# Two-block transformer kernel on one core: where the big SBUF tiles start, and how far apart the weight buffers lie

## Chip, cores and metric

The kernel runs on 1 core of one Trainium2 chip. The metric is the device time of one launch in microseconds (us). Three runs of the kernel before took 925.46, 927.27 and 922.51 us; the median is 925.46 us.

## What is computed

256 tokens of width 1024 pass through two different transformer blocks, all in float32. Cut to what matters here:

```python
def reference(x, ...):
    # block 1: sliding-window attention (8 heads) and retention (4 heads), gated, then an MLP
    proj = rmsnorm(x) @ w_in
    ...
    h = x + (ga * (y_a @ w_att_up) + gr * (y_r @ w_ret_up)) @ w_out
    x = rmsnorm(h + square(relu(rmsnorm(h) @ w_ff1)) @ w_ff2)
    # block 2: 16 meta tokens in front; windowed attention (16 heads) and differential attention
    ...
    h = h + rms_norm((g_swa * (o_swa @ w_bs) + g_diff * (o_diff @ w_bd)) @ w_out_2)
    u = rms_norm(h)
    return h + rms_norm((silu(u @ w_gate) * (u @ w_up)) @ w_ffn_out)
```

There are some 36 million weights. They are used once each, so the kernel is one long stream of weights past a small set of activations.

## The kernel before

**Units.** The host packs all weights, in the order of their use, into 272 units of 128 partitions x 1024 float32 (512 KB each). `fetch` (L285 to L302) brings in one unit. SyncE's queue loads it into a tile `raw` (4 buffers). ScalarE copies it into `hi` (L299, two pieces of 512 columns), rounded to the format fp32r, and VectorE writes the remainder `lo = raw - hi` (L301, two pieces). `hi` and `lo` have five buffers each (`WB = 5`), taken in turn. `next_unit` keeps one unit ahead of the one in use. A few units go into big activation tiles that are free at that time (`spare`), and are then called `w`.

**Products.** Activations are kept split in the same way: a big tile such as `x1t` holds, for each of 8 slices k of the contraction, a hi part and a lo part. One product is three fp32r matmuls (`PASS`): hi by hi, hi by lo, lo by hi. A matmul has a stationary operand, which a weight load brings into the array (128 columns, 512 bytes in each partition), and a moving operand, which streams past it. There are two large kinds:

- `mm_a` (L454): the unit's 128x128 slices are stationary and 256 token columns of the activation move (1,024 bytes in each partition; 272 columns in block 2's attention, with the meta tokens). 24 matmuls per unit. Its activations are `x1t`, `xf1t`, `x2t`, `xf2t`, `ret_t`, `oa_t`, `os_t`, `od_t`.
- `mm_b` (L466): 128 tokens of the activation are stationary (`m1t`, `m2t`, `hid`) and 512 columns of the unit move (2,048 bytes). 12 matmuls per unit. `mm_group` (L476) does the same for a group of four units.

A slice k of a big tile follows the last at 1,024 bytes. Only `x2t` has 272 columns to a slice, so that its slices follow at 1,088 bytes.

Transposes go through TensorE too (L433, L580, L961 and others), with the data as stationary and a 128x128 identity as the moving operand. A few products (L689 to L691, L973 to L975) are in plain float32.

**SBUF.** The pools stand one behind the other in each partition: `const` (small tables, `vec` among them), `w` (the weight buffers), `big` (the big activation tiles), `small`, and then one pool per phase. A pool rounds a tile's size up to 32 bytes. So the size of `vec`, 40 floats or 160 bytes, sets where all that comes behind it starts. `consts2` (L361) makes `vec`, and borrows a `raw` buffer for the masks (L364).

**Order.** The scheduler of the framework sets the order of each engine's instructions; the change leaves it as it is.

Of the kernel before, what the change touches and what calls it, by code (L numbers as in the profile page):

```python
# [9 lines left out]
F32 = mybir.dt.float32  # L10
F32R = mybir.dt.float32r
# [5 lines left out]
P = 128  # L17
# [5 lines left out]
EPS = 1e-6  # L23
MASKED = 1e30
UC = 1024

RET_H = 4

# [2 lines left out]
WB = 5  # L31
# [192 lines left out]
class Body:  # L224
# [59 lines left out]
    def fetch(self):  # L284
        nc = self.nc  # L285
        u = self.un
        self.un += 1
        if u in self.place:
            hi, lo = self.place.pop(u)
        else:  # L290
            hi = self.wp.tile([P, UC], F32R, tag="hi", bufs=WB, name=f"hi{u}")
            lo = self.wp.tile([P, UC], F32R, tag="lo", bufs=WB, name=f"lo{u}")
        raw = self.wp.tile([P, UC], F32, tag="raw", bufs=4, name=f"raw{u}")
        nc.sync.dma_start(out=raw, in_=self.io["wstream"][u])
        if self.hi_pool:
            nc.gpsimd.tensor_scalar(out=hi, in0=raw, scalar1=1.0, scalar2=0.0, op0=ALU.mult, op1=ALU.add)
        else:
            for c in range(0, UC, PIECE):
                nc.scalar.copy(hi[:, c:c + PIECE], raw[:, c:c + PIECE])  # L299
        for c in range(0, UC, PIECE):  # L300
            nc.vector.tensor_sub(lo[:, c:c + PIECE], raw[:, c:c + PIECE], hi[:, c:c + PIECE].bitcast(F32))  # L301
        self.ready.append((hi, lo))  # L302

    def spare(self, skip, tags):

        u = self.un + skip
        for tag in tags:
            if tag == "DE":
                self.place[u] = [self.bp.tile([P, UC], F32R, tag="D", name=f"hi{u}"),
                                 self.bp.tile([P, UC], F32R, tag="E", name=f"lo{u}")]  # L310
# [50 lines left out]
    def consts2(self):  # L361
        nc, cp, io = self.nc, self.cp, self.io
        cc = _CC
        mk = self.wp.tile([P, UC], F32, tag="raw", bufs=4, name="mk")[:, 0:3 * P]  # L364
        a, n = cc["masks"]
        nc.sync.dma_start(out=mk, in_=io["consts"][:, a:a + n])
        self.identb = cp.tile([P, P], BF16, name="identb")
        self.masks = cp.tile([P, 3 * P], BF16, name="masksb")
        nc.gpsimd.tensor_copy(self.identb, self.ident)
        nc.gpsimd.tensor_copy(self.masks, mk)  # L370
        self.vec = cp.tile([P, 40], F32, name="vec")
        nc.sync.dma_start(out=self.vec, in_=io["vec"])
        self.hb = cp.tile([P, 32], F32, name="hb")
        nc.gpsimd.tensor_scalar(out=self.hb, in0=self.vec[:, 0:32], scalar1=0.5, scalar2=None, op0=ALU.mult)
        rb = cp.tile([P, 24 + 256 + P], F32, name="rows")
        nc.sync.dma_start(out=rb, in_=io["rows"].broadcast_to([P, 280 + P]))
        self.nsink = cp.tile([P, 24], F32, name="nsink")
        nc.gpsimd.tensor_scalar(out=self.nsink, in0=rb[:, 0:24], scalar1=-1.0, scalar2=None, op0=ALU.mult)
        self.sub = rb[:, 280:]
        nc.gpsimd.tensor_scalar(out=self.sub, in0=self.sub, scalar1=0.8, scalar2=None, op0=ALU.mult)  # L380
        lam4 = rb[:, 24:280].rearrange("p (a b d) -> p a b d", a=2, b=2)
        pr = cp.tile([P, 2, 64], F32, name="lampr")
        nc.gpsimd.tensor_tensor(out=pr, in0=lam4[:, :, 0, :], in1=lam4[:, :, 1, :], op=ALU.mult)
        s2 = cp.tile([P, 2], F32, name="lams")
        nc.vector.reduce_sum(out=s2, in_=pr, axis=AX.X)
        e2 = cp.tile([P, 2], F32, name="lame")
        nc.scalar.activation(out=e2, in_=s2, func=AF.Exp)
        self.nlam = cp.tile([P, 1], F32, name="nlam")
        nc.gpsimd.tensor_tensor(out=self.nlam, in0=e2[:, 1:2], in1=e2[:, 0:1], op=ALU.subtract)
        nc.gpsimd.tensor_scalar(out=self.nlam, in0=self.nlam, scalar1=-(0.8 - 0.6 * math.exp(0.0)), scalar2=None,  # L390
                                op0=ALU.add)
# [740 lines left out]
```

## Time and profile before

| | |
|---|---|
| median of 3 runs | 925.46 us (922.51 to 927.27) |
| profiled execution, its own time | 926.7 us |
| its span (first to last instruction) | 924.9 us |
| TensorE matmul busy (PE) | 896.0 us, 97% |
| TensorE weight load busy (PEld) | 819.9 us, 89% |
| VectorE busy (DVE) | 627.7 us, 68% |
| ScalarE busy (ACT) | 516.5 us, 56% |
| GpSimd busy (POOL) | 174.7 us, 19% |
| weights and tables from HBM | 151.83 MB, 166 GB/s over the span |

Matmuls are pipelined: one starts while the last is still under way, so the duration of one (283 ns for 256 columns) is longer than the distance from start to start. In this text that distance is called the *pitch*. It is read from the timeline: the start of one row, the start of a later row, and the number of matmuls between them. In a row of the timeline "x2" means two equal instructions in a run, with the start of the first.

### The profile page before, as it was taken

The numbers are of one execution on the slowest core, as the hardware profiler recorded it, in microseconds if no ns is written. First come the engines' busy times: TensorE is split into PE (matmuls) and PEld (weight loads), VectorE is DVE, ScalarE is ACT, GpSimd is POOL, SyncE is SP. The second block draws the span as 40 slices with busy tenths as digits, with TensorE's granted clock in tenths as the row PEclk, the third lists the DMA queues.
The fourth block names the chain that finished last, engine by engine and source line by source line (L and its number), as shares of the span: only waits on it lengthen the run. The fifth ranks groups of instructions, "written<-read, shape, count | busy, mean of one in ns | idle before, by whom it ended". The sixth has DMA issues, their size and how long they took to land. (4 is left out here: it accounts for less than half of the span.)

```text
span 924.9 us, 16482 instructions
## 1 busy us (share of the span) xinstructions
PE 896.0 (97%) x6188; PEld 819.9 (89%) x6188; DVE 627.7 (68%) x1201; ACT 516.5 (56%) x1128; POOL 174.7 (19%) x181
## 2 busy tenths in 40 slices
PE   6999899999999999999989999999999999999997
PEld 4898889998899999987989878899999799999996
DVE  5556789667755544575589999988567675655554
ACT  4544367555554445565557778886455464444442
POOL 3013460101001111001273534451011100000000
PEclk9999999999999999999999999999999999999999
DMA  8675544478565565662564333433466666666651
GB/s 280 232 207 167 154 150 137 123 220 294 174 209 190 185 182 183 189 220 94 189 207 135 110 110 127 138 109 115 136 184 209 224 206 191 189 190 182 183 159 45
DMA packets 48126, 160.18 MB, mean 173 GB/s; under 512 B 6432, under 2 KB 8224, under 8 KB 48048
## 3 DMA queue, kind: packets, MB, share of 16 engines
q1 hardware_dynamic: 43376, 153.95, 52.6%
q10 hardware_dynamic: 4672, 5.20, 2.0%
q8 instruction: 48, 0.79, 0.3%
q14 instruction: 30, 0.25, 0.1%
HBM read 151.83 MB, written 2.10 MB: 166 GB/s over the span
## 5 line engine op out<-in xcount | busy, mean ns | idle before, releaser
L301 DVE TENSOR_TENSOR lo<-raw,hi 128x512 fp32r<-128x512 f32 x536 | 380.5, 751 | 195.1 <-ACT hi L299 190.5
L299 ACT CAST hi<-raw 128x512 fp32r<-128x512 f32 x532 | 301.9, 618 | 244.3 <-issue 84.7
L466 PE MATMUL op<-hi,hid 128*128 128x512 f32 x416 | 131.1, 396 | 0.0
L454 PE MATMUL fi_ps<-xf2t,hi 128*128 128x256 f32 x640 | 115.7, 283 | 0.0
L454 PEld LDWEIGHTS fi_ps<-xf2t,hi 128*128 128x128 f32 x640 | 100.4, 192 | 1.0
L466 PEld LDWEIGHTS op<-hi,hid 128*128 128x128 f32 x416 | 76.4, 188 | 16.4
L454 PE MATMUL fi_ps<-xf2t,lo 128*128 128x256 f32 x320 | 90.5, 283 | 0.0
L466 PE MATMUL op<-lo,hid 128*128 128x512 f32 x208 | 82.0, 396 | 0.0
L454 PE MATMUL f_ps<-xf1t,hi 128*128 128x256 f32 x448 | 81.3, 283 | 0.0
L454 PEld LDWEIGHTS f_ps<-xf1t,hi 128*128 128x128 f32 x448 | 70.7, 191 | 1.4
L454 PE MATMUL f_ps<-xf1t,lo 128*128 128x256 f32 x224 | 63.3, 282 | 0.0
L454 PEld LDWEIGHTS fi_ps<-xf2t,lo 128*128 128x128 f32 x320 | 61.3, 192 | 0.0
L454 PE MATMUL q_ps<-x2t,hi 128*128 128x256 f32 x256 | 50.4, 287 | 0.4 <-ACT t L503 0.4
L454 PE MATMUL gate_ps<-x1t,hi 128*128 128x256 f32 x256 | 49.1, 287 | 0.0
L454 PE MATMUL gate_ps<-x2t,hi 128*128 128x256 f32 x256 | 48.7, 285 | 0.0
L466 PEld LDWEIGHTS op<-lo,hid 128*128 128x128 f32 x208 | 39.1, 188 | 9.4
L415 POOL TENSOR_SCALAR e<-ss 128x1 f32<-128x1 f32 (+1 forms) x11 | 4.0, 362 | 223.9 <-ACT py L1028 195.0
L795 POOL TENSOR_TENSOR sq<-relu 128x512 f32<-128x512 f32 x14 | 15.8, 1132 | 152.0 <-ACT relu L792 152.0
L454 PEld LDWEIGHTS f_ps<-xf1t,lo 128*128 128x128 f32 x224 | 42.8, 191 | 0.1
L454 PEld LDWEIGHTS q_ps<-x2t,hi 128*128 128x128 f32 x256 | 40.4, 189 | 1.5 <-ACT t L503 0.6
L454 PEld LDWEIGHTS gate_ps<-x2t,hi 128*128 128x128 f32 x256 | 40.0, 189 | 0.6 <-issue 0.5
L454 PEld LDWEIGHTS gate_ps<-x1t,hi 128*128 128x128 f32 x256 | 40.3, 191 | 0.2
(297 smaller groups left out, 2023.8 us busy)
## 6 DMA issues: line engine op xcount, KB each, us to landing
raw<-in_wstream_dram SPq DMA_DIRECT2D x272, 512.0 KB, 3.6
sw<-t ACTq DMA_DIRECT2D x40, 64.0 KB, 3.8
x<-in_x_dram SPq DMA_DIRECT2D x3, 512.0 KB, 6.0
sw<-t ACTq DMA_DIRECT2D x40, 34.0 KB, 2.4
sw<-t ACTq DMA_DIRECT2D x8, 128.0 KB, 5.0
g_pre<-in_gains_dram SPq DMA_DIRECT2D x2, 512.0 KB, 6.1
x<-hf SPq DMA_DIRECT2D x2, 512.0 KB, 2.8
x<-x SPq DMA_DIRECT2D x2, 512.0 KB, 6.1
```

The source lines that it names most:

```text
L299: nc.scalar.copy(hi[:, c:c + PIECE], raw[:, c:c + PIECE])
L301: nc.vector.tensor_sub(lo[:, c:c + PIECE], raw[:, c:c + PIECE], hi[:, c:c + PIECE].bitcast(F32))
L415: nc.gpsimd.tensor_scalar(out=e[:np_], in0=ss[:np_, 0:1], scalar1=1.0 / D, scalar2=EPS, op0=ALU.mult, op1=ALU.add)
L454: nc.tensor.matmul(out, wv[a][:, k, j * P:(j + 1) * P], XT[:, b, k, n0:n1], start=(i == 0), stop=(i == last))
L466: nc.tensor.matmul(out, XT[:, b, k0 + k, t0:t1], wv[a][:, k, c0:c0 + cn], start=(start and i == 0), stop=(stop and i == last))
L795: nc.gpsimd.tensor_tensor(out=q, in0=r, in1=r, op=ALU.mult)
```

## The change

`vec` gets 48 columns instead of 40 (the DMA still fills 40), so that everything behind it moves by 32 bytes. The weight buffers `hi`, `lo` and `raw` get 1,040 columns instead of 1,024, of which the first 1,024 are used, so that one buffer follows the next at 4,160 bytes instead of 4,096. Nothing else changes: in the built program the rows of all five engines, with their waits and buffer numbers, are the same as before, but for the line numbers (the lines behind L25 move down by one, those from L371 on by two).

```diff
 UC = 1024
+UP = UC + 16
...
         else:
-            hi = self.wp.tile([P, UC], F32R, tag="hi", bufs=WB, name=f"hi{u}")
-            lo = self.wp.tile([P, UC], F32R, tag="lo", bufs=WB, name=f"lo{u}")
-        raw = self.wp.tile([P, UC], F32, tag="raw", bufs=4, name=f"raw{u}")
+            hi = self.wp.tile([P, UP], F32R, tag="hi", bufs=WB, name=f"hi{u}")[:, 0:UC]
+            lo = self.wp.tile([P, UP], F32R, tag="lo", bufs=WB, name=f"lo{u}")[:, 0:UC]
+        raw = self.wp.tile([P, UP], F32, tag="raw", bufs=4, name=f"raw{u}")[:, 0:UC]
...
-        mk = self.wp.tile([P, UC], F32, tag="raw", bufs=4, name="mk")[:, 0:3 * P]
+        mk = self.wp.tile([P, UP], F32, tag="raw", bufs=4, name="mk")[:, 0:3 * P]
...
-        self.vec = cp.tile([P, 40], F32, name="vec")
-        nc.sync.dma_start(out=self.vec, in_=io["vec"])
+
+        self.vec = cp.tile([P, 48], F32, name="vec")
+        nc.sync.dma_start(out=self.vec[:, 0:40], in_=io["vec"])
```

The two programs' tables of addresses (bytes from the start of a partition; the remainders are what the text speaks of):

| tile | before | remainder by 64, by 256 | changed | remainder by 64, by 256 |
|---|---|---|---|---|
| `hi`, five buffers | 20704, 24800, 28896, 32992, 37088 | 32, 224 for all | 20736, 24896, 29056, 33216, 37376 | 0; 0, 64, 128, 192, 0 |
| `lo`, five buffers | 41184 to 57568, 4096 apart | 32, 224 for all | 41536 to 58176, 4160 apart | 0; 64, 128, 192, 0, 64 |
| `raw`, four buffers | 61664 to 73952, 4096 apart | 32, 224 for all | 62336 to 74816, 4160 apart | 0; 128, 192, 0, 64 |
| `x1t`, `xf1t`, `od_t` | 78048 | 32, 224 | 78976 | 0, 128 |
| `m1t`, `m2t`, `os_t` | 94432 | 32, 224 | 95360 | 0, 128 |
| `ret_t`, `x2t`, `xf2t` | 110816 | 32, 224 | 111744 | 0, 128 |
| `hid`, four places | 180768, 184864, 188960, 193056 | 32, 32 | 181696, 185792, 189888, 193984 | 0, 192 |
| `p` (five buffers), `a` (two) | 200864 and on, 1120 apart | 32 and 0 in turn | 201792 and on | 0 and 32 in turn |
| `ident` (transposes) | 16512 | 0, 128 | 16512 | 0, 128 |

While one matmul streams its moving operand, the weights of the next are loaded. The *distance* below is the address of a matmul's moving operand less that of the stationary operand loaded for the next one, its remainder by 256. Over the 5,691 matmuls in fp32r it stands so in the two programs:

| moving columns | program | 0 | 64 | 128 | 192 |
|---|---|---|---|---|---|
| 256 | before | 3325 | 210 | 200 | 259 |
| 256 | changed | 820 | 1045 | 1247 | 874 |
| 272 | before | 128 | 139 | 127 | 118 |
| 272 | changed | 134 | 125 | 106 | 116 |
| 512 | before | 454 | 33 | 0 | 657 |
| 512 | changed | 245 | 316 | 331 | 271 |

(The 272 wide rows have the odd difference at the ends of runs. A handful of narrower matmuls is not shown.) Before, the 256 wide ones at other distances than 0 are those of `x2t`, whose slices are 1,088 bytes apart and so go through all four distances; of the 512 wide ones at 192, 622 are those of `hid`.

## Rows read from the trace of the kernel before

**Rows 1.** The page: span and busy time of each engine.

```profile
span 924.9 us, 16482 instructions
PE 896.0 (97%) x6188; PEld 819.9 (89%) x6188; DVE 627.7 (68%) x1201; ACT 516.5 (56%) x1128; POOL 174.7 (19%) x181
```

**Rows 2.** Busy time by stretch, core 0: stretch, its us, busy us (instructions).

```profile
core 0: us, PE busy (x) PEld busy (x) DVE busy (x) ACT busy (x) POOL busy (x), PEclk, DMA share, GB/s
0.00:50.00 50.00, 41.18 (x218) 35.15 (x219) 27.61 (x45) 25.17 (x49) 9.51 (x19) 1.00 0.76 259
...
250.00:420.00 170.00, 170.00 (x1049) 150.93 (x1048) 95.05 (x153) 88.32 (x163) 17.29 (x18) 1.00 0.62 196
...
450.00:640.00 190.00, 182.41 (x1373) 166.27 (x1373) 170.15 (x375) 142.99 (x367) 88.86 (x77) 1.00 0.44 130
...
735.00:905.00 170.00, 169.95 (x1192) 158.54 (x1190) 101.11 (x185) 82.12 (x164) 0.00 (x0) 1.00 0.57 177
```

**Rows 3.** Timeline of PE, a stretch of `mm_a`, `xf2t` moving: start, us, what.

```profile
897.31 0.40 PE L454 MATMUL fi_ps<-xf2t,hi 128*128 128x256 f32 x2
897.55 0.28 PE L454 MATMUL fi_ps<-xf2t,lo 128*128 128x256 f32 x1
897.67 0.40 PE L454 MATMUL fi_ps<-xf2t,hi 128*128 128x256 f32 x2
...
902.71 0.40 PE L454 MATMUL fi_ps<-xf2t,hi 128*128 128x256 f32 x2
```

**Rows 4.** Timeline of PEld in the same stretch: the weight loads.

```profile
897.20 0.31 PEld L454 LDWEIGHTS fi_ps<-xf2t,hi 128*128 128x128 f32 x2
897.43 0.19 PEld L454 LDWEIGHTS fi_ps<-xf2t,lo 128*128 128x128 f32 x1
897.55 0.31 PEld L454 LDWEIGHTS fi_ps<-xf2t,hi 128*128 128x128 f32 x2
```

**Rows 5.** Timeline of PE, a stretch of `mm_a` with `x2t` moving.

```profile
671.85 0.40 PE L454 MATMUL gate_ps<-x2t,hi 128*128 128x256 f32 x2
672.09 0.28 PE L454 MATMUL gate_ps<-x2t,lo 128*128 128x256 f32 x1
672.21 0.40 PE L454 MATMUL gate_ps<-x2t,hi 128*128 128x256 f32 x2
...
676.47 0.40 PE L454 MATMUL gate_ps<-x2t,hi 128*128 128x256 f32 x2
```

**Rows 6.** Timeline of PE, `mm_b` with `m2t` stationary.

```profile
719.44 0.61 PE L466 MATMUL op<-hi,m2t 128*128 128x512 f32 x2
719.89 0.39 PE L466 MATMUL op<-lo,m2t 128*128 128x512 f32 x1
...
724.20 0.61 PE L466 MATMUL op<-hi,m2t 128*128 128x512 f32 x2
```

**Rows 7.** Timeline of PE, `mm_b` with `hid` stationary.

```profile
275.95 0.63 PE L466 MATMUL op<-hi,hid 128*128 128x512 f32 x2
276.42 0.39 PE L466 MATMUL op<-lo,hid 128*128 128x512 f32 x1
...
280.85 0.63 PE L466 MATMUL op<-hi,hid 128*128 128x512 f32 x2
```

**Rows 8.** Timeline of PE, `mm_group` with `x2t` stationary, 512 columns moving.

```profile
424.68 0.39 PE L476 MATMUL vb_ps<-hi,x2t 128*128 128x512 f32 x1
...
427.67 0.39 PE L476 MATMUL vb_ps<-lo,x2t 128*128 128x512 f32 x1
```

**Rows 9.** Two tiles' instructions: duration ns min/median/max, first and last start.

```profile
L961 PEld LDWEIGHTS at_ps<-ident,a x32: 138/141/143, 589.4 to 654.2; 128*128 128x128 f32 x32
L939 ACT ACTIVATE p<-s,mn x32: 474/488/526, 560.3 to 648.2; 128x272 f32<-128x272 f32 x32
```

**Rows 10.** Timeline of PE, transposes of the two `a` buffers in turn.

```profile
599.64 0.49 PE L961 MATMUL at_ps<-ident,a 128*128 128x128 f32 x3
599.97 0.27 PE L966 MATMUL atm_ps<-ident,a 128*16 128x128 f32 x1
```

**Rows 11.** Timeline of PE, plain float32 products, 256 columns moving.

```profile
77.04 0.59 PE L689 MATMUL ro<-vr,at 128*128 128x256 f32 x2
77.47 0.59 PE L690 MATMUL ro<-vr,at 128*128 128x256 f32 x2
77.90 0.59 PE L691 MATMUL ro<-vr,at 128*128 128x256 f32 x2
```

**Rows 12.** Splitting on VectorE, one stretch: duration ns min/median/max; and `hid`.

```profile
L301 DVE TENSOR_TENSOR lo<-raw,hi x7: 678/685/1782, 700.8 to 711.9; 128x512 fp32r<-128x512 f32 x7
L328 DVE TENSOR_TENSOR hid<-sq,hid x14: 682/683/693, 257.8 to 404.9; 128x512 fp32r<-128x512 f32 x14
```

## Prediction

> **What bounds the kernel now.** First the page: TensorE's matmuls are busy for 896.0 of 924.9 us, VectorE for 68%, ScalarE for 56% [rows 1]. Then the busy time by stretch: in the MLP stretches (250 to 420 us, 735 to 905 us) PE has no idle time that counts, while VectorE has 95 of 170 us and 101 of 170 us [rows 2]. Only 450 to 640 us (block 2's attention) has another engine close behind: VectorE 170 of 190 us, PE 182. [...] So the time is the number of matmuls times their pitch, and this change, which moves no instruction, can act only through the pitch, or through an engine's time for the same instruction.
>
> The reader is to look at the pitch next. With `xf2t` moving it is (902.71 − 897.31)/45 = 120.0 ns for 256 columns [rows 3]; with `m2t` stationary (724.20 − 719.44)/21 = 226.7 ns for 512 columns [rows 6]. [...]
>
> Two rows show that addresses take part. With `x2t` moving the pitch is (676.47 − 671.85)/39 = 118.5 ns, same operation, same shape [rows 5]; its distances go through all four values, those of `xf2t` are all 0. With `hid` stationary it is (280.85 − 275.95)/21 = 233.3 ns against 226.7 for `m2t` [rows 6, 7]; their distances are 192 and 0. And where the stationary `x2t` goes through the four distances at 512 columns, it is (427.67 − 424.68)/13 = 230.0 ns [rows 8]. I read these as two reads of one engine, the moving operand and the next weights, that get in each other's way, by an amount that depends on where they stand to each other.
>
> [...]
>
> **The change, part by part.**
>
> *Nothing is added or moved.* Order, waits and DMAs are the same. The 16 columns per buffer are never written or read.
>
> *The 64 bytes between the weight buffers.* They spread the distances: of the 256 wide matmuls 820 instead of 3,325 stay at distance 0, the rest go to all others, about as in `x2t`. I price the new mixture by `x2t`, the nearest row: 120.0 − 118.5 = 1.5 ns, times 3,325: −5.0 us. The 512 wide ones now stand in a mixture too, 230.0 ns by [rows 8]: 657 at distance 192 gain 3.3 ns each, −2.2 us; 454 at distance 0 lose 3.3 ns, +1.5 us. Sum −5.7 us.
> The bounds: a unit keeps one distance for its 24 matmuls, while `x2t` changes it every three, and it may be the change that helps. Then the price of a fixed unequal distance is that of `hid`, +6.6 ns over distance 0 [rows 6, 7], and it is the bound above. Below, no 256 wide matmul can come under its weight load: transposes, which do little else, follow at (599.97 − 599.64)/3 = 110 ns [rows 10]; that is 10 ns on 3,325, 33 us. I take `x2t`, because it has the same line, shape and mixture.
>
> *The start at a multiple of 64 instead of 32 past one.* Three rows say nothing happens. `p` and `a` lie at remainder 32 and 0 in turn, and ScalarE's 32 writes of `p` are at 488 ns in the middle [rows 9]; the 32 weight loads from `a` all take 138 to 143 ns [rows 9], and the transposes that alternate between both follow at an even 110 ns [rows 10]. VectorE's split takes 685 ns with its tiles all at the same remainder, and 683 ns on `hid`, which stands elsewhere [rows 12]. [...] So I price it at 0, with a bound below of one 64-byte piece per matmul (the second rival).
>
> *VectorE, ScalarE, DMA.* 0. The spread of the rows above is some 2 ns on 544 splits, 1 us on an engine that is idle for a third of the time; that cover is thinnest from 450 to 640 us, where most matmuls are of `x2t` and change nothing anyway. No row shows a DMA's address; where PE is full the DMA engines are busy for 0.57 to 0.62 of the time, at 177 to 196 GB/s [rows 2], so a better landing is hidden, and a worse one too until a third more is asked of them.
>
> *Sum.* 926.7 (the profiled execution's own time) − 5.7 = 921.0 us. That execution is 1.2 us over the median of 925.46; against the median the sum is **919.8 us**, 0.6% less. PE is the bound nearly everywhere where distances change, so I take nothing off for what others hide. From no change a measurement of this kernel tells about 0.5%, 4.6 us: below 920.8 is faster, above 930.1 slower.
>
> **The rivals.**
>
> *Fixed distances cost as `hid` does* (slower). 2,505 of the 256 wide matmuls leave distance 0, in units that stay at one other distance for 24 matmuls; at +6.6 ns, 16.5 us. 209 of the 512 wide ones leave it too, +1.4 us; those of `hid` that stay off 0 gain nothing. 925.5 + 17.9 = 943 us; at half that price 934. It decides from a mean of +1.9 ns per matmul that leaves distance 0 on, 4.6 us over 2,505. For it: [rows 7], the only long run at a fixed unequal distance, is the slowest. Against it: at 256 columns `x2t`'s three matmuls at each distance show no such cost [rows 5]. Chance 0.16.
>
> *The start counts in pieces of 64 bytes* (much faster). [...] A moving row of 1,024 bytes that starts 32 bytes past a multiple of 64 touches 17 pieces of 64 bytes, not 16. If the operand is fetched in such pieces at just the rate at which it is used, the extra one costs 16 columns, 6.7 ns, and the change takes it away from all 5,691 fp32r matmuls: 38 us, 919.8 − 38 = 882 us. With half of it hidden, 901. [...] Chance 0.25.
>
> *Addresses change nothing* (925.5 us, within 2). What a unit gains at one distance it loses at another, and the start is indifferent. [...] Chance 0.17.
>
> **How the numbers follow.** The forecast, only the distances count and a mixture costs as in `x2t`, has 0.42; it spans 915 to 924, by some 4 us for the price of the mixture, and 0.6 of it lies below 920.8. Faster: 0.25 + 0.42 × 0.6 = 0.50. Same: 0.17 + 0.42 × 0.4 = 0.34. Slower: 0.16. The range goes from 888 to 936: it takes in the forecast, no change, the slow rival up to above half its price and the fast one but for its lower end; what is left out is about 0.08 on each side. The forecast's own range is 915 to 924.
>
> **What would show it.** Right: pitch of `mm_a` with `xf1t` or `xf2t` moving near 118.5 ns in the mean over several units, different from unit to unit; `mm_b` with `hid` near 230; `x2t` still 118.5; transposes 110, ScalarE's and VectorE's durations as before. The fast rival: `x2t` too falls, to some 112 ns, and the 512 wide ones to 224 or less. The slow one: `xf2t` at 124 to 127 in three units of four. Wrong in its ground would be a PE that shows the predicted pitch and waits for VectorE or a DMA in its place.

## The result, and the profile after

The changed kernel takes 917.86 us in the median of 10 runs (915.97 to 920.5), the kernel before 923.79 us in the median of 10 (922.12 to 927.27): a ratio of 0.9938, 95% interval 0.9927 to 0.995. It is 0.6% faster. 919.8 us was forecast, from the earlier median of 925.46: the same 0.6%.

The page of the changed kernel, span and busy time, answers to [rows 1]:

```profile
span 914.4 us, 16482 instructions
PE 888.0 (97%) x6188; PEld 813.1 (89%) x6188; DVE 626.2 (68%) x1201; ACT 516.0 (56%) x1128; POOL 174.5 (19%) x181
```

The busy time by stretch answers to [rows 2]. PE is full in the MLP stretches as before, and the granted clock is 1.00 there in both kernels.

```profile
core 0: us, PE busy (x) PEld busy (x) DVE busy (x) ACT busy (x) POOL busy (x), PEclk, DMA share, GB/s
250.00:420.00 170.00, 170.00 (x1050) 149.52 (x1048) 94.16 (x152) 89.50 (x167) 18.23 (x22) 1.00 0.61 195
735.00:905.00 170.00, 170.00 (x1203) 158.94 (x1202) 99.63 (x183) 80.20 (x161) 0.00 (x0) 1.00 0.56 177
```

PE lost 8.0 us of busy time, VectorE 1.5 and ScalarE 0.5. PE is still 97% of a shorter span: the same matmuls follow each other more closely.

How closely is read best in block 2's MLP, which repeats one pattern: four units of `mm_a` with `xf2t` moving (96 matmuls of 256 columns), then `mm_b` with `hid` stationary (24 of 512). The start of each part is enough. Timeline of PE, changed kernel, where each part begins (the rows between are left out):

```profile
851.89 0.40 PE L456 MATMUL fi_ps<-xf2t,hi 128*128 128x256 f32 x2
...
863.16 0.63 PE L468 MATMUL op<-hi,hid 128*128 128x512 f32 x2
...
868.74 0.40 PE L456 MATMUL fi_ps<-xf2t,hi 128*128 128x256 f32 x2
...
880.01 0.62 PE L468 MATMUL op<-hi,hid 128*128 128x512 f32 x2
...
885.54 0.40 PE L456 MATMUL fi_ps<-xf2t,hi 128*128 128x256 f32 x2
...
896.91 0.63 PE L468 MATMUL op<-hi,hid 128*128 128x512 f32 x2
```

The three parts with `xf2t` take 11.27, 11.27 and 11.37 us, 117.4, 117.4 and 118.4 ns per matmul, 117.7 in the mean, against 120.0 in [rows 3]. The two with `hid` take 5.58 and 5.53 us, 232.5 and 230.4 ns, against 233.3 in [rows 7]. With the five buffers at different remainders, one part is no longer like the next.

The three parts are a fair sample. Over the whole of both timelines, the 256 wide steps (from one matmul's start to the next) of all big tiles but `x2t` fell from 119.6 to 117.8 ns in the mean, those of `hid` from 233.5 to 231.9.

Two more stretches of the same timeline: 48 matmuls with `x2t` moving (a pair of units between two of `od_t`), and 21 with `m2t` stationary.

```profile
674.56 0.41 PE L456 MATMUL gate_ps<-x2t,hi 128*128 128x256 f32 x2
...
680.21 0.40 PE L456 MATMUL bd_ps<-od_t,hi 128*128 128x256 f32 x2
...
711.03 0.62 PE L468 MATMUL op<-hi,m2t 128*128 128x512 f32 x2
...
715.86 0.62 PE L468 MATMUL op<-hi,m2t 128*128 128x512 f32 x2
```

`x2t` now stands at (680.21 − 674.56)/48 = 117.7 ns (118.5 in [rows 5]), `m2t` at (715.86 − 711.03)/21 = 230.0 ns (226.7 in [rows 6]). And what the change should leave alone: weight loads of `a`, ScalarE's writes of `p`, VectorE's split, in the tables of their tiles (minimum, median, maximum in ns).

```profile
L963 PEld LDWEIGHTS at_ps<-ident,a x32: 138/141/143, 581.5 to 646.2; 128*128 128x128 f32 x32
...
L941 ACT ACTIVATE p<-s,mn x30: 476/487/529, 559.6 to 640.2; 128x272 f32<-128x272 f32 x30
...
L302 DVE TENSOR_TENSOR lo<-raw,hi x10: 676/685/1785, 695.1 to 707.8; 128x512 fp32r<-128x512 f32 x10
```

Medians 141, 487 and 685 ns, before 141, 488 and 685 [rows 9, 12].

### The profile page after: what moved, and what is told of

Same layout as the page of the kernel before. It is cut to its first block, busy times and chain, and to the rows that moved or that the text cites. A ratio compares the mean times of both kernels' runs of the same rounds, so it can differ in the third digit from the quotient of the medians.

```text
span 914.4 us, 16482 instructions
## 1 busy us (share of the span) xinstructions
PE 888.0 (97%) x6188; PEld 813.1 (89%) x6188; DVE 626.2 (68%) x1201; ACT 516.0 (56%) x1128; POOL 174.5 (19%) x181
## 5 line engine op out<-in xcount | busy, mean ns | idle before, releaser
L456 PE MATMUL fi_ps<-xf2t,hi 128*128 128x256 f32 x640 | 113.8, 281 | 0.0
```

The costliest lines, as they stand in the source:

```text
L456: nc.tensor.matmul(out, wv[a][:, k, j * P:(j + 1) * P], XT[:, b, k, n0:n1], start=(i == 0), stop=(i == last))
```

## The experiments

Three theories stand against each other. **D**: what counts is the distance between a matmul's moving operand and the weights loaded beside it. **A**: what counts is where an operand starts. **M**: what counts is that the weight buffers no longer all stand at one remainder, whatever moves. While the runs came in, a fourth joined: **P**, a run of matmuls can settle in either of two paces.

### Each half of the change by itself

Only the start (`e1`): the lines of `vec`, and nothing else.

```diff
-        self.vec = cp.tile([P, 40], F32, name="vec")
-        nc.sync.dma_start(out=self.vec, in_=io["vec"])
+        self.vec = cp.tile([P, 48], F32, name="vec")
+        nc.sync.dma_start(out=self.vec[:, 0:40], in_=io["vec"])
```

> Only the start moves by 32 bytes (vec 48 columns), so weights and big tiles start at multiples of 64; the weight buffers stay 4,096 bytes apart, every distance stays as before. Theory D (only the distance counts): same time as before, ratio 0.998 to 1.002; xf2t 120 ns per matmul of 256 columns, hid 233 per 512. Rival A (the start counts): the whole gain is here, ratio about 0.994, xf2t about 118. Rival M (what counts is that hi and lo buffers no longer stand at the same remainder, whatever moves): ratio 1.000.

Measured: ratio 0.9995 (0.998 to 1.001), no difference. Timeline of PE, the pattern of the MLP:

```profile
877.39 0.39 PE L454 MATMUL fi_ps<-xf2t,hi 128*128 128x256 f32 x2
...
888.89 0.63 PE L466 MATMUL op<-hi,hid 128*128 128x512 f32 x2
...
894.49 0.39 PE L454 MATMUL fi_ps<-xf2t,hi 128*128 128x256 f32 x2
```

11.50/96 = 119.8 ns and 5.60/24 = 233.3 ns, as before. This half of the change is worth nothing, and theory A has fallen as far as a start at 32 or 0 past a multiple of 64 goes.

Only the spacing (`e2`): the change with `vec` left at 40 columns.

```diff
+UP = UC + 16
...
-            hi = self.wp.tile([P, UC], F32R, tag="hi", bufs=WB, name=f"hi{u}")
+            hi = self.wp.tile([P, UP], F32R, tag="hi", bufs=WB, name=f"hi{u}")[:, 0:UC]
...
```

> Only the 64 bytes between the weight buffers; all starts stay at 32 past a multiple of 64. Theory D: as the whole change, ratio 0.992 to 0.996, xf2t between 117 and 118.5 from unit to unit. Rival A: 1.000 and xf2t 120. Rival M: as the whole change.

Measured: ratio 0.9937 (0.9916 to 0.9957), the whole change's 0.9938.

```profile
871.15 0.40 PE L456 MATMUL fi_ps<-xf2t,hi 128*128 128x256 f32 x2
...
882.42 0.62 PE L468 MATMUL op<-hi,hid 128*128 128x512 f32 x2
...
887.95 0.40 PE L456 MATMUL fi_ps<-xf2t,hi 128*128 128x256 f32 x2
```

117.4 ns and 230.4 ns: the same as in the changed kernel. All of the gain lies in the spacing.

### One distance for all

These runs go back to the kernel before, with all weight buffers 4,096 bytes apart and at one remainder, and put an unused tile ahead of the big tiles. So the 256 wide matmuls stand at one distance again, only at another one (those of `x2t` still go through several). All pools behind the big tiles move along, `hid` with them. The edit, here for 64 bytes (16 columns); the other runs have 32, 128, 160, 192 and 224 bytes:

```diff
         self.bp = pool("big")
+        self.bp.tile([P, 16], F32, tag="pad", name="pad")
```

> The kernel before with 64 unused bytes ahead of the big tiles: weight buffers stay 4,096 bytes apart, all starts stay at 32 past a multiple of 64, but the 256 wide matmuls stand at the one distance 64 (3,329 of them), hid's at 128, m1t's and m2t's at 192. Theory D: xf2t near 117.5 ns in every unit, hid near 231, m2t 232 to 233; sum 3,300 x -2.2 = -7.3, hid 587 x -2.5 = -1.5, others 390 x +5 = +2.0 us: -6.8 us, ratio 0.9925 (0.991 to 0.995). Rival A: 1.000. Rival M (all weight buffers keep one remainder): 1.000, xf2t 120.

Measured: ratio 0.9959 (0.9946 to 0.9971).

```profile
870.86 0.40 PE L455 MATMUL fi_ps<-xf2t,hi 128*128 128x256 f32 x2
...
882.16 0.63 PE L467 MATMUL op<-hi,hid 128*128 128x512 f32 x2
...
887.76 0.40 PE L455 MATMUL fi_ps<-xf2t,hi 128*128 128x256 f32 x2
```

`xf2t` at 117.7 ns without any spread among the weight buffers: M, for which the spread was needed, has fallen, and D had its number. `hid` at distance 128 is at 233.3 ns, where D had 231, which is a part of why the gain is smaller than the expected 0.9925.

> As the one with 64, with 192 unused bytes: the 256 wide at distance 192 (3,377), hid at 0 (612), the other 512 wide at 64 (365). Theory D: xf2t near 117.5 ns, hid 227 instead of 233 (the value that m2t has at distance 0 in the kernel before), m2t 231 to 233 instead of 227; -7.3 - 4.0 + 1.8 = -9.5 us, ratio 0.990 (0.987 to 0.993). Rivals A and M: 1.000. Should hid stay at 233 although at distance 0, the distance is not what sets the pitch at 512 columns.

Measured: ratio 0.9863 (0.9846 to 0.9881), more than twice the gain of the change. The same pattern, and above it two units of `qr_ps` with `x1t` moving (48 matmuls), early in block 1:

```profile
54.24 0.39 PE L455 MATMUL qr_ps<-x1t,hi 128*128 128x256 f32 x2
...
59.68 0.39 PE L455 MATMUL gr_ps<-x1t,hi 128*128 128x256 f32 x2
...
864.45 0.40 PE L455 MATMUL fi_ps<-xf2t,hi 128*128 128x256 f32 x2
...
875.76 0.62 PE L467 MATMUL op<-hi,hid 128*128 128x512 f32 x2
...
881.20 0.40 PE L455 MATMUL fi_ps<-xf2t,hi 128*128 128x256 f32 x2
```

`hid`, now at distance 0, fell to 5.44/24 = 226.7 ns, exactly what `m2t` had at distance 0 in the kernel before [rows 6]: the distance makes those 6.6 ns, not the tile. `xf2t` is at 117.8 ns, as expected. But `x1t`, at the same distance, runs at 5.44/48 = 113.3 ns. One distance has two paces, and it is not the tile that decides: `xf1t` lies at `x1t`'s address and runs, but for the first of its 26 units, at 117.8 ns, and `x1t` itself has four units at 117.8. This was not expected, and it is where the extra gain comes from.

> As the ones with 64 and 192 unused bytes, with 128: the 256 wide at distance 128 (3,306), hid at 64 (587), the other 512 wide at 128 (372). Theory D (a pitch belongs to each distance): xf2t near 118.2 ns (x2t's mean at that distance), hid 229 to 230 (as m2t at 64 in the run with 192), m2t 233 (as hid at 128 in the run with 64): -1.4 x 3.3 - 4.0 x 0.59 + 5 x 0.37 = -5.1 us, ratio 0.9945 (0.992 to 0.997). Rival P (the pace depends also on the state in which a run of matmuls begins, as x1t's 113.3 and xf2t's 117.7 ns at the one distance 192 suggest): two paces again, in whole units.

Measured: ratio 0.9977 (0.9963 to 0.9991).

```profile
875.37 0.40 PE L455 MATMUL fi_ps<-xf2t,hi 128*128 128x256 f32 x2
...
886.89 0.62 PE L467 MATMUL op<-hi,hid 128*128 128x512 f32 x2
...
892.40 0.40 PE L455 MATMUL fi_ps<-xf2t,hi 128*128 128x256 f32 x2
```

`hid` at 64 is at 229.6 ns, as D had it. `xf2t` at 128 is at 120.0 ns, where D had 118.2 from `x2t`'s single steps: a miss. But two units of `x1t`, at the same distance, take less in this run:

```profile
55.42 0.40 PE L455 MATMUL qr_ps<-x1t,hi 128*128 128x256 f32 x2
...
61.12 0.40 PE L455 MATMUL gr_ps<-x1t,hi 128*128 128x256 f32 x2
```

That is 5.70/48 = 118.8 ns, and nearly all units of `x1t`, `ret_t`, `oa_t` and `od_t` stay there: two paces again, in whole units, as P had it. Nor does a distance cost alone what it costs among others: over the whole timeline of the kernel before, `x2t`'s steps at distance 0 take 118.0 ns in the mean, `xf2t`'s, all at 0, 119.8.

> 32 unused bytes: the big tiles now start at multiples of 64 while the weights stay 32 past one; the 256 wide at distance 32 (3,294), hid at 160, the other 512 wide at 224. If the distance counts in steps of 64 bytes: xf2t either 120.0 or 117.8, hid 233.3, m2t 227 or 233; ratio 1.000 or 0.994. If it counts in smaller steps: xf2t, hid and m2t at values that no distance so far has shown. The start itself should again count for nothing, though here only the moving tile is aligned.

Measured: ratio 0.9954 (0.993 to 0.9979).

```profile
869.92 0.39 PE L455 MATMUL fi_ps<-xf2t,hi 128*128 128x256 f32 x2
...
881.12 0.63 PE L467 MATMUL op<-hi,hid 128*128 128x512 f32 x2
...
886.73 0.40 PE L455 MATMUL fi_ps<-xf2t,hi 128*128 128x256 f32 x2
```

116.7 ns at distance 32: neither the 119.8 of distance 0 nor the 117.7 of 64. The distance counts in steps smaller than 64 bytes. (Steps smaller than 32 were not tried.) From the big tiles on, `e1` and this run have the same addresses; of the operands of the large matmuls only the weight buffers lie elsewhere, by 32 bytes. So the 3.1 ns between the two runs (119.8 and 116.7) come from where the weights lie to the moving tile, and not from where that tile starts.

This distance has a second pace too. `x1t` runs at 116.7 ns early in block 1, and later, over two units:

```profile
180.29 0.40 PE L455 MATMUL gate_ps<-x1t,hi 128*128 128x256 f32 x2
...
185.94 0.40 PE L455 MATMUL gate_ps<-x1t,hi 128*128 128x256 f32 x2
```

That is 5.65/48 = 117.7 ns.

> 224 unused bytes: the 256 wide at distance 224 (3,293), hid at 224 (637), the other 512 wide at 32. In steps of 64 bytes: the 256 wide as at 192 (113.3 to 117.7 ns) or as at 0 (120), hid 233 or 227; so ratio between 0.993 and 1.003. In smaller steps: other values, and the time could lie under that of the run with 192 (0.986).

Measured: ratio 0.9973 (0.9959 to 0.9986). `xf2t` at 11.36/96 = 118.3 ns, a value of its own again, `hid` at 5.60/24 = 233.3 ns.

```profile
873.07 0.40 PE L455 MATMUL fi_ps<-xf2t,hi 128*128 128x256 f32 x2
...
884.43 0.63 PE L467 MATMUL op<-hi,hid 128*128 128x512 f32 x2
...
890.03 0.40 PE L455 MATMUL fi_ps<-xf2t,hi 128*128 128x256 f32 x2
```

> 160 unused bytes: the 256 wide at distance 160 (3,298), hid at 32 (615), the other 512 wide at 96. From the single steps of x2t in the runs with 32 and 224 unused bytes, which stand at 118.9 ns at that distance: xf2t 118.9, hid 233.3 (as m2t at 32 there); -0.8 x 3.3 = -2.6 us and +1.9 from m1t, m2t and x1t if they go to some 232: ratio 0.998 to 1.001. If a pitch can't be carried over from x2t's mixture, xf2t lies elsewhere between 113 and 120.

Measured: ratio 0.9971 (0.9953 to 0.9989), a little better than expected. The parts of its MLP pattern take 11.39 and 5.59 us: 118.6 ns (118.9 expected) and 232.9 ns. `x1t` is at 117.3 ns over two units early in block 1 (54.64 to 60.27 us): a second pace at this distance as well, which explains a part of the better time.

### What decides between the two paces

The next two runs keep the 192 bytes, and so the distance of all 256 wide matmuls, and move the pools behind the big tiles by an unused tile ahead of them (16 columns for `e8`, 48 for `e9`). Of the operands of the MLP's matmuls that moves `hid` alone:

```diff
         self.sp = pool("small")
+        self.sp.tile([P, 16], F32, tag="pads", name="pads")
```

> The run with 192 unused bytes, and 64 more ahead of the phase pools, so that hid goes back from distance 0 to 192 while all 256 wide matmuls keep 192. Theory D: hid back at 233.4 ns (+4 us against the run with 192: ratio 0.990 to 0.991), x1t and xf2t unchanged at 114.7 and 117.6 in the mean. Rival P: xf1t and xf2t, which follow on runs of hid, change to the other pace, 113.3 ns (-7 us, ratio 0.983), as the state that hid leaves behind is another one; x1t, ret_t and od_t, which follow on no run of hid, keep theirs.

Measured: ratio 0.9873 (0.9854 to 0.9892). Timeline of PE, two rounds of the pattern:

```profile
848.68 0.40 PE L456 MATMUL fi_ps<-xf2t,hi 128*128 128x256 f32 x2
...
859.99 0.62 PE L468 MATMUL op<-hi,hid 128*128 128x512 f32 x2
...
865.59 0.40 PE L456 MATMUL fi_ps<-xf2t,hi 128*128 128x256 f32 x2
...
876.49 0.62 PE L468 MATMUL op<-hi,hid 128*128 128x512 f32 x2
...
882.08 0.40 PE L456 MATMUL fi_ps<-xf2t,hi 128*128 128x256 f32 x2
...
893.39 0.62 PE L468 MATMUL op<-hi,hid 128*128 128x512 f32 x2
```

The parts with `xf2t` take 11.31, 10.90 and 11.31 us: 117.8, 113.5 and 117.8 ns, in turn. Same tiles, same instructions, same distance; only what went before differs. (The matmuls' output banks are the same in every round of the pattern, the three buffers of `hid` come round in three rounds and the five weight buffers in five, while the paces alternate by two through the whole MLP.) `hid` is back at (865.59 − 859.99)/24 = 233.3 ns. So D's rise for `hid` and a part of P's fall for `xf2t` came together, and nearly cancel (0.9873 against 0.9863).

> The run with 192 unused bytes, and 192 more ahead of the phase pools, so that hid goes from distance 0 to 64; all 256 wide matmuls keep 192. Theory D alone: hid 229.7 instead of 227.0 ns (as in the run with 128 unused bytes), +1.6 us on the run with 192: ratio 0.988; xf1t and xf2t stay at 117.6. With rival P (a run of matmuls can settle in either of two paces, 113.3 or 117.7 ns, and the run of hid before it decides which): xf1t and xf2t again in another share of the two, as in the run with hid at 192, where half of the units went at 113.3; all at 113.3 would be -7 us, ratio 0.980.

Measured: 907.65 us, ratio 0.982 (0.9802 to 0.9838).

```profile
859.40 0.40 PE L456 MATMUL fi_ps<-xf2t,hi 128*128 128x256 f32 x2
...
870.31 0.62 PE L468 MATMUL op<-hi,hid 128*128 128x512 f32 x2
...
875.80 0.40 PE L456 MATMUL fi_ps<-xf2t,hi 128*128 128x256 f32 x2
```

`xf2t` at 10.91/96 = 113.6 ns, `hid` at 5.49/24 = 228.8 ns. `hid` is 2.1 ns slower than at distance 0, but what follows on it settles in the faster pace. D alone (0.988) is excluded by the interval, P is borne out. This is the fastest version: 1.8% under the kernel before, almost three times the gain of the change, and its interval lies wholly under that of the change. Its page:

```profile
span 904.0 us, 16482 instructions
PE 875.4 (97%) x6188; PEld 802.2 (89%) x6188; DVE 627.4 (69%) x1201; ACT 516.0 (57%) x1128; POOL 174.6 (19%) x181
```

PE has 875.4 us of busy time against 888.0 in the changed kernel, VectorE 627.4 against 626.2: the gain is again all in the pitch.

All one-distance runs together (pitches in the MLP pattern, ns):

| unused bytes ahead of the big tiles | distance of `xf2t`: pitch | distance of `hid`: pitch | ratio to before |
|---|---|---|---|
| 0 (start moved only, `e1`) | 0: 119.8 | 192: 233.3 | 0.9995 |
| 32 | 32: 116.7 | 160: 233.8 | 0.9954 |
| 64 | 64: 117.7 | 128: 233.3 | 0.9959 |
| 128 | 128: 120.0 | 64: 229.6 | 0.9977 |
| 160 | 160: 118.6 | 32: 232.9 | 0.9971 |
| 192 | 192: 117.8 | 0: 226.7 | 0.9863 |
| 192, `hid` 64 further | 192: 117.8 and 113.5 in turn | 192: 233.3 | 0.9873 |
| 192, `hid` 192 further | 192: 113.6 | 64: 228.8 | 0.982 |
| 224 | 224: 118.3 | 224: 233.3 | 0.9973 |

The pitches of `xf2t` are one pace of each distance. `x1t` shows another at 128 (118.8), 160 (117.3), 32 (117.7) and 192 (113.3); with 64 and 224 unused bytes all units of the tiles at that distance stay within half a ns of each other.

## Why the prediction was right

**What bounds the kernel.** Right: only the pitch changed, PE stayed at 97% of the span, and nothing else took over.

**The start at a multiple of 64, priced at 0.** Right, by `e1`: 0.9995. The rival that the start counts in pieces of 64 bytes is out. Its 6.7 ns for 16 columns agree with an estimate from the rows: 256 more columns take 226.7 − 120.0 = 106.7 ns [rows 3, 6], a sixteenth of which is 6.7. But no run shows an extra piece at that price: with the starts at a multiple of 64 `xf2t` stays at 119.8 ns (`e1`), and in `e4` `x1t` runs at 113.3 ns, 6.7 under the 120.0 of [rows 3], with its start still 32 past one.

**The 256 wide matmuls, −5.0 us.** Right in kind, sized a little low: over the whole of both timelines they fell by 119.64 − 117.78 = 1.86 ns, or 5.9 us over the 3,141 steps that follow each other without a wait in both. The price taken from `x2t`, 1.5 ns, was too small. That no 256 wide matmul can come under the 110 ns at which the transposes follow [rows 10] was an estimate; no run shows what sets such a limit, only that none of the 256 wide steps of `mm_a` is under 112 ns before and 111 ns in the changed kernel.

The picture behind the price was off as well. The prediction has a unit keep one distance for its 24 matmuls. But by the table of addresses a unit's `lo` buffer lies 64 bytes past its `hi` buffer in the remainder, so that in the changed kernel a unit goes through two distances. And it has 820 matmuls that stay at distance 0, as if they kept their pitch: `xf2t`'s steps at distance 0, 119.8 ns in the mean before, take 117.9 in the changed kernel, at 64, 128 and 192 they take 116.9, 118.3 and 117.8. So the gain of the change is not a sum of prices that belong to the distances; that a mixture is cheaper than distance 0 alone is shown, what it costs was borrowed from a like row.

**The 512 wide ones, −2.2 and +1.5 us.** The second was nearly hit: `m2t` went from 226.7 to 230.0 ns, and all of this kind together lost 1.2 us. The first was halved: `hid` fell from 233.5 to 231.9 ns over the whole of both timelines, not to 230, −1.1 us. (In the kernel before, the table of distances should have 19 and not 0 at 512 columns and distance 128, nearly all of them `x2t`'s, which does go through all four.)

**`x2t`, priced at 0.** Wrong by a little: 118.5 to 117.7 ns in the stretches shown, −0.7 us over all its moving steps, the 272 wide ones included. Its distances are as mixed as before, but its `hi` and `lo` weights now stand at different remainders; that this is the reason was not tried by itself.

**The sum.** By these terms −5.9 − 1.1 + 1.2 − 0.7 = −6.5 us; the medians say −5.9 (923.79 to 917.86), and −5.7 was forecast. PE's busy time says −8.0, but the two profiled executions differ by more than the medians (926.7 and 916.17): the one before lay 2.9 us above its ten runs' median and the one after 1.7 below. The sum is better than its terms, and that is luck: `hid` gained 1.1 us less than forecast, the 256 wide matmuls and `x2t` 1.6 us more.

**The slow rival, that fixed distances cost as `hid` does.** Wrong for 256 columns: no tile that keeps one distance runs above 120.0 ns in any of the runs, and distance 0 is itself among the dearest. It was half right for 512 columns: with one distance for all, 0 is the cheapest there (226.7), 64 next (228.8 to 229.6), and the others that `hid` had are at 232.9 to 233.8. So the same address relation is bad for one width and good for the other, which the argument from `hid` to `xf2t` left out.

**No effect of addresses.** Out by `e2` (ratio 0.9937) and `e4` (0.9863): the runs show 226.7 to 233.8 ns for one shape, 512 columns, by the place of the tiles alone. Its half on the start agrees with `e1` (0.9995).

That two reads of one engine get in each other's way remains the reading, not a finding: the runs show that the relation of the two addresses changes the pitch, together with what ran before, and not by what means.

## What to carry to other kernels

When TensorE is full (here 97% of the span), compare the pitch of equal matmuls from place to place before looking for work to remove: a few ns that differ with nothing but the tiles' addresses are a sign that the layout can be tuned, here for up to 1.8%. Spreading the weight buffers left a mixture of paces (units of `xf2t` between 116.5 and 119.6 ns in the changed kernel); placing moving tiles and weights at one good distance (here 192 for 256 columns, 0 or 64 for 512) gave more than twice as much (1.4% in `e4` and 1.8% in `e9`, against 0.6%). Move one pool at a time by 32 or 64 unused bytes and read the pitch of each kind of matmul, because the best distance differs by width, as here, and because one distance can have two paces (117.8 and 113.5 ns in turn in `e8`) that differ by what ran before.

## What the hardware showed that was not expected

At distance 192, 256 wide fp32r matmuls have two steady paces: 113.3 ns in `e4`'s `x1t`, 117.8 in its `xf2t`. In `e8` the same loop takes them in turn, four units at 117.8 (11.31 us) and four at 113.5 (10.90 us), and keeps each until the run of `hid` in between. The run of `hid` before it takes part in which one it is: with `hid` at distance 0 (`e4`) all units of `xf2t` but the first are at the slow pace, at 64 (`e9`) all but one at the fast one, at 192 (`e8`) both come in turn, after runs of `hid` of the same pitch. I read this as something that is handed on through the run of `hid`; no run shows what it would be.

Other distances have two paces too, closer together: 118.8 and 120.0 ns at 128, 116.7 and 117.7 at 32, 117.3 and 118.6 at 160. At 64 and 224 these runs show only one. Whether a second one is there, and whether a layout could be had in which all tiles go at 113.3 ns, was not tried.
